# Eight state space groups in one rotation, attention masks made in the layer before, a norm emitted sooner

## The chip, the cores and the metric

The kernel runs on one core of one Trainium2 chip. The metric is the device time of one execution in microseconds (us). Five engines run side by side, each in its own fixed order of instructions: TensorE (PE, matmuls), VectorE (DVE), ScalarE (ACT), GpSimd (POOL) and SyncE (SP, which here only issues DMAs). They wait for each other by semaphores. POOL and ACT issue DMAs too, in their own instruction order.

## The reference

One layer of a decoder, for 1024 prompt tokens and 8 sample tokens that share the weights:

```
x += 1/2 * SwiGLU(RMSNorm(x))                # first FFN: 1024 -> 2816 -> 1024
h  = RMSNorm(x);  [u | q | k | v | gates] = h @ w_in
A  = S5 state space branch of u (32 groups of 16 channels, 64 complex states each), then a GLU
B  = dilated sliding window attention of q, k, v: (window, dilation) = (128,1), (512,4), (2048,16)
x += (sigmoid(gate_ssm) * (A @ w_ssm_proj) + sigmoid(gate_attn) * (B @ w_attn_proj)) @ w_o
x += 1/2 * SwiGLU(RMSNorm(x))                # second FFN
```

All in fp32. It also returns the updated key/value windows and states. The state space branch needs, for each group, tables of the powers of its 64 complex poles; they depend on weights alone. The attention needs two masks, which depend on nothing but positions.

## The kernel before

Tokens are columns: 1032 of them in three chunks of CH = 344. Features lie on the partitions, so x is three tiles xT of 128 x 8 x 344. A product in fp32 is made of three matmuls on high and low parts (`ah`/`al`, cast by ACT and subtracted by DVE, `parts` L1188).

The stages run in this order: load and first norm (`load_x` L846, nine blocks of rows: eight of 128 prompt rows, the last of 8 sample rows), first FFN up, first FFN down (`ffn_down(0)`), the mixing stage (`mix` L931: w_in products, state space, attention), the output projection and second FFN. The FFN layers use a Strassen-like scheme; its products are named P1 to P7, d1, d2, `lo` and `hi`, and each ends in four evictions on DVE (L1524) that add half of the product to xT.

Beside the products of `ffn_down(0)` the tables of the state space branch are made: after every third product `run` (L1526) calls `ssm_tables`. Its first call makes the poles (`ssm_poles` L172, many small DVE instructions on scratch tiles, result in `PO`). Each of eight further calls makes the powers for four groups on POOL, a rotation: R[128, 4, 2, 128] is filled by seven doubling steps of six instructions (L351 to L356), behind two copies (L344, L345), and is stored to DRAM (`r_d`, L358) by a DMA that POOL issues. R has one buffer, so the next rotation waits for that DMA. The call also makes other tables for the same groups on DVE and PE (L365 to L395). `ssm_inputs` (L262) makes HA, the sample states times a power, and SP stores it (`ha_d`, L315).

The masks are made by `att_setup` (L505) at the start of `mix`, in tiles of a pool of its own: one iota on POOL (L511), eight DVE instructions (L512 to L519).

The norm between the stages is `wo_norm` (L1193), once per chunk. It copies xT to DRAM (`x_d`, L1197, issued by POOL), squares on ACT (L1202, L1205), adds on DVE (L1206), sums over partitions by a matmul with ones (L1210), takes the reciprocal root (ACT L99 to L101, DVE L102 to L107), scales xT in place (L1214, which can only write when the copy to x_d has read the tile) and makes the parts for the first mixing products (L1190, L1191, then PE at L136). The w_in weights are loaded by SP (L117) into two buffers r, cast by ACT (L121) and split by DVE (L122); the next load waits for the split.

The written program gives dependences and the pools' buffers; the order on each engine is set by a scheduler that simulates the program (`schedule_with_timeline_sim=True`). So code that moves in the text shifts instructions on all engines.

## Time and profile before

| | |
|---|---|
| median of 3 runs | 2431.03 us (2425.07 to 2433.76) |
| the profiled execution | 2429.43 us, its span 2427.3 us |
| mean granted TensorE clock | 0.968 of full |
| busy: PE, DVE, ACT, POOL | 2261.9 (93%), 1559.8 (64%), 892.5 (37%), 320.5 us (13%) |

The profile is one execution. The page has the busy time of each engine, the span in 40 slices (a digit is the busy share in tenths) and the costliest groups of instructions. The timeline lists instructions with start and length; in brackets is how long the engine stood idle before one and what released it. The windows give each engine's busy time in chosen stretches. The engine with the highest share is not busy in every stretch, so one looks for the stretches where it stands.

### The profile page before, as it was taken

The numbers are of one execution on the slowest core, as the hardware profiler recorded it, in microseconds if no ns is written. First come the engines' busy times: TensorE is split into PE (matmuls) and PEld (weight loads), VectorE is DVE, ScalarE is ACT, GpSimd is POOL, SyncE is SP. The second block draws the span as 40 slices with busy tenths as digits, with TensorE's granted clock in tenths as the row PEclk, the third lists the DMA queues.
The fourth block names the chain that finished last, engine by engine and source line by source line (L and its number), as shares of the span: only waits on it lengthen the run. The fifth ranks groups of instructions, "written<-read, shape, count | busy, mean of one in ns | idle before, by whom it ended". The sixth has DMA issues, their size and how long they took to land.

```text
span 2427.3 us, 36784 instructions
## 1 busy us (share of the span) xinstructions
PE 2261.9 (93%) x14013; PEld 2162.4 (89%) x14013; DVE 1559.8 (64%) x3206; ACT 892.5 (37%) x1624; POOL 320.5 (13%) x594
## 2 busy tenths in 40 slices
PE   5999999999998079999999999899999999999999
PEld 4999999998997079987888788799999999998999
DVE  7766666679987354465557444567876666664664
ACT  6433333342221234455444443234533333333222
POOL 1000010100687710000000000120010101000000
PEclk9999999999999589999999999999999999999999
DMA  5455554577865337763143125668243434367543
GB/s 192 148 168 197 169 189 157 189 264 284 281 233 184 122 93 212 212 189 96 37 114 93 39 70 155 196 238 260 94 146 117 146 112 142 117 239 266 202 162 133
DMA packets 321830, 403.92 MB, mean 166 GB/s; under 512 B 40294, under 2 KB 266966, under 8 KB 318710
## 3 DMA queue, kind: packets, MB, share of 16 engines
q1 hardware_dynamic: 290294, 220.58, 29.8%
q0 software_dynamic: 26816, 128.54, 14.6%
q10 hardware_dynamic: 4544, 52.45, 6.3%
q8 instruction: 110, 1.80, 0.3%
q14 instruction: 66, 0.54, 0.1%
HBM read 282.62 MB, written 162.88 MB: 184 GB/s over the span
## 4 chain that ended last, share of the span: by engine, by line
PE 57%; issue 12%; DMA 11%; DVE 8%; POOL 7%; ACT 2%; SPq 2%; POOLq 0%; DVEq 0%; ACTq 0%
PE pm L1302 27%; PE pm L136 16%; PE pm L1533 9%; DMA r<-in_w_o_dram 2%; PE ps L601 2%; POOL R L356 1%; POOL q L354 1%; POOL R L353 1%; DMA r_d<-R 1%; DVE xT L1214 1%; DVE w L1191 1%; POOL q L355 1%; DMA al<-hs_d 1%; POOL hs_d L1330 1%; DMA r<-in_w_in_dram 1%
## 5 line engine op out<-in xcount | busy, mean ns | idle before, releaser
L136 PE MATMUL pm<-ah,w 128*128 128x344 f32 x1776 | 464.3, 329 | 18.9 <-ACT ah L1190 15.0
L136 PE MATMUL pm<-al,w 128*128 128x344 f32 x1632 | 439.1, 329 | 19.9 <-ACT al L1190 10.9
L1190 ACT CAST w<-r 128x1024 fp32r<-128x1024 f32 (+1 forms) x253 | 240.0, 949 | 547.6 <-PE pm L1302 349.4
L1302 PE MATMUL pm<-ah,w 128*128 128x344 f32 x2376 | 403.2, 322 | 1.0 <-ACT ah L1190 1.0
L1302 PEld LDWEIGHTS pm<-ah,w 128*128 128x128 f32 x2376 | 383.4, 190 | 1.3 <-ACT ah L1190 1.3
L136 PEld LDWEIGHTS pm<-ah,w 128*128 128x128 f32 x1776 | 315.0, 190 | 33.0 <-ACT ah L1190 15.6
L1191 DVE TENSOR_TENSOR w<-r,w 128x1024 fp32r<-128x1024 f32 (+1 forms) x253 | 277.1, 1096 | 91.1 <-ACT w L1190 90.7
L136 PEld LDWEIGHTS pm<-al,w 128*128 128x128 f32 x1632 | 294.1, 192 | 31.5 <-ACT al L1190 11.9
L1302 PE MATMUL pm<-e,w 128*128 128x344 f32 x1584 | 268.3, 322 | 14.4 <-ACT e L1190 13.4
L1302 PE MATMUL pm<-al,w 128*128 128x344 f32 x1584 | 273.9, 322 | 2.5 <-ACT p L1385 2.5
L1302 PEld LDWEIGHTS pm<-e,w 128*128 128x128 f32 x1584 | 254.5, 189 | 14.9 <-ACT e L1190 13.5
L1302 PEld LDWEIGHTS pm<-al,w 128*128 128x128 f32 x1584 | 255.7, 189 | 3.0 <-ACT p L1385 2.8
L1330 POOL DMA_DIRECT2D hs_d<-hs x110 | 75.1, 682 | 888.5 <-DVE hs L1191 840.7
L1533 PE MATMUL pm<-al,w 128*128 128x344 f32 x1068 | 183.1, 323 | 2.1 <-DVE ah L1524 2.1
L1533 PEld LDWEIGHTS pm<-al,w 128*128 128x128 f32 x1068 | 171.1, 190 | 3.7 <-DVE ah L1524 2.4
L122 DVE TENSOR_TENSOR w<-r,w 128x1024 fp32r<-128x1024 f32 (+1 forms) x58 | 60.6, 1044 | 87.0 <-ACT w L121 86.5
L1533 PE MATMUL pm<-al,x 128*128 128x344 f32 x636 | 110.9, 325 | 5.4 <-ACT ah L1541 5.0
L1533 PEld LDWEIGHTS pm<-al,x 128*128 128x128 f32 x636 | 103.1, 192 | 6.8 <-ACT ah L1541 5.3
L1127 POOL DMA_DIRECT2D rs<-g_d x24 | 12.9, 542 | 527.5 <-issue 390.4
L121 ACT CAST w<-r 128x1024 fp32r<-128x1024 f32 (+1 forms) x58 | 52.1, 898 | 74.7 <-PE pm L136 44.1
L1190 ACT CAST hs<-h 128x688 fp32r<-128x688 f32 (+1 forms) x66 | 44.1, 670 | 73.9 <-DMA hs_d<-hs 73.9
L1533 PE MATMUL pm<-e,x 128*128 128x344 f32 x360 | 65.0, 331 | 4.8 <-DVE x L1191 2.5
(427 smaller groups left out, 3279.9 us busy)
## 6 DMA issues: line engine op xcount, KB each, us to landing
hs_d<-hs POOLq DMA_DIRECT2D x88, 688.0 KB, 4.5
out_dram<-in_cache_kv_w_dram ACTq DMA_DIRECT2D x64, 512.0 KB
r<-in_w_gate_dram SPq DMA_DIRECT2D x44, 512.0 KB
r<-in_w_up_dram SPq DMA_DIRECT2D x44, 512.0 KB
al<-hs_d SPq DMA_DIRECT2D x21, 1032.0 KB
r<-in_w_in_dram SPq DMA_DIRECT2D x38, 512.0 KB
r<-in_w_down_dram SPq DMA_DIRECT2D x30, 512.0 KB
x_d<-xT POOLq DMA_DIRECT2D x9, 1376.0 KB, 7.1
```

The lines of the kernel that those rows point to most:

```text
L121: nc.scalar.copy(h[:, :k], raw[:, :k])
L122: nc.vector.tensor_sub(l[:, :k], raw[:, :k], h[:, :k])
L136: nc.tensor.matmul(p, w[:, kw], a[:, ka], start=first and i == 0, stop=last and i == n - 1)
L353: P.tensor_sub(CR[:, :, L:2 * L], q1[:, :, :L], q2[:, :, :L])
L354: P.tensor_mul(q1[:, :, :L], CR[:, :, :L], bi)
L355: P.tensor_mul(q2[:, :, :L], CI[:, :, :L], br)
L601: nc.tensor.matmul(p[h][:, :nk], qT[hs, s.block(g, b)], kT[hs, ks], start=True, stop=True)
L1190: s.nc.scalar.copy(hi, x)
L1191: s.nc.vector.tensor_sub(lo, x, hi)
L1302: nc.tensor.matmul(p, W[w][:, k], B[:, a, k], start=first and k == 0 and z == 0, stop=k == n - 1 and z == 2, skip_group_check=True)
L1330: nc.gpsimd.dma_start(s.hs_d[i:i + n, j].rearrange("i p z n -> p i (z n)"), t[:, :n].rearrange("p i z n -> p i (z n)").bitcast(F32))
L1533: nc.tensor.matmul(p[m], W[wz][:, m], t[:, jj, az], start=e == 0 and k == 0, stop=e == n - 1 and k == 2, skip_group_check=True)
```

## The change

- Rotations: only odd calls of `ssm_tables` make one, for eight groups: R[128, 8, 2, 128], 2 copies and 48 instructions (the last doubling step in two pieces of 32), one DMA of twice the bytes. Four batches replace eight.
- The poles' scratch and HA move into R's one buffer.
- `att_setup` is called at the start of `ffn_down(0)` and uses tiles rs0 to rs2 of its pool.
- `normed(0)`, the first chunk's norm, is emitted ahead of the product P3.
- `load_x` takes the sample rows seventh of nine.

```diff
--- before.py
+++ after.py
@@ -173,7 +173,16 @@
 
         nc, i = s.nc, s.i
         V = nc.vector
-        t, _ = s.ssm_pools(tp, tp)
+        RT = tp.tile([128, 8, 2, 128], F32, name="R", bufs=1).rearrange("p a b c -> p (a b c)")
+        at = [0]
+
+        def t(sh, dt=F32):
+            n = math.prod(sh[1:])
+            x = RT[:sh[0], at[0]:at[0] + n]
+            at[0] += n
+            x = x if dt == F32 else x.bitcast(dt)
+            return x if len(sh) == 2 else x.rearrange("p (a b) -> p a b", a=sh[1])
+
         s.poles(tp)
 
         a2 = t([32, 2, 128])
@@ -209,7 +218,7 @@
         V.memset(PW[:, 1, 0], 0.0)
         V.tensor_mul(PW[:, 0, 1], mag, cs)
         V.tensor_mul(PW[:, 1, 1], mag, sn)
-        m1, m2 = (tp.tile([128, 4, 64], F32, name=f"q{z}", bufs=1)[:, :, :32] for z in (1, 2))
+        m1, m2 = (tp.tile([128, 8, 32], F32, name=f"q{z}", bufs=1)[:, :4] for z in (1, 2))
 
         def cmul(outr, outi, ar, ai, br, bi, n):
             V.tensor_mul(m1[:, :n], ar, br)
@@ -295,7 +304,7 @@
         nc.sync.dma_start(s.dv, i['ssm_d'].rearrange("o (g c) -> c (o g)", c=16))
         hre = i['state_ssm_re'][0].rearrange("b g p -> (b g) p").rearrange("(q r) p -> q r p", q=2)
         him = i['state_ssm_im'][0].rearrange("b g p -> (b g) p").rearrange("(q r) p -> q r p", q=2)
-        HA = tp.tile([128, 2, 8, 32], F32, name="HA")
+        HA = tp.tile([128, 8, 2, 128], F32, name="R", bufs=1)[:, 0:2].rearrange("p a b c -> p (a b c)").rearrange("p (z b g) -> p z b g", z=2, b=8)
         HT = t(2, 256).rearrange("p (b g) -> p b g", b=8)
         for q in range(2):
             hn = t(q, 192)
@@ -337,25 +346,29 @@
             nm = names[g0 // 2 % 2][z]
             return tmp.tile([128, CH], F32, name=nm, bufs=2 if nm == "sq" else 1)[:, :sh]
 
-        sl = slice(4 * n - 4, 4 * n)
-        R = tp.tile([128, 4, 2, 128], F32, name="R", bufs=1)
-        q1, q2 = tp.tile([128, 4, 64], F32, name="q1", bufs=1), tp.tile([128, 4, 64], F32, name="q2", bufs=1)
-        CR, CI = R[:, :, 0], R[:, :, 1]
-        P.tensor_copy(CR[:, :, 0], s.ER[:, 3, sl])
-        P.tensor_copy(CI[:, :, 0], s.EI[:, 3, sl])
-        L = 1
-        while L < 128:
-            sh = [128, 4, L]
-            q = 3 + L.bit_length() - 1
-            br, bi = s.ER[:, q, sl, None].to_broadcast(sh), s.EI[:, q, sl, None].to_broadcast(sh)
-            P.tensor_mul(q1[:, :, :L], CR[:, :, :L], br)
-            P.tensor_mul(q2[:, :, :L], CI[:, :, :L], bi)
-            P.tensor_sub(CR[:, :, L:2 * L], q1[:, :, :L], q2[:, :, :L])
-            P.tensor_mul(q1[:, :, :L], CR[:, :, :L], bi)
-            P.tensor_mul(q2[:, :, :L], CI[:, :, :L], br)
-            P.tensor_add(CI[:, :, L:2 * L], q1[:, :, :L], q2[:, :, :L])
-            L *= 2
-        nc.gpsimd.dma_start(s.r_d[:, sl], R)
+        if n % 2:
+            sl = slice(4 * n - 4, 4 * n + 4)
+            R = tp.tile([128, 8, 2, 128], F32, name="R", bufs=1)
+            CR, CI = R[:, :, 0], R[:, :, 1]
+            P.tensor_copy(CR[:, :, 0], s.ER[:, 3, sl])
+            P.tensor_copy(CI[:, :, 0], s.EI[:, 3, sl])
+            L = 1
+            while L < 128:
+                q = 3 + L.bit_length() - 1
+                for l0 in range(0, L, 32):
+                    k = min(L, 32)
+                    sh = [128, 8, k]
+                    a, o = slice(l0, l0 + k), slice(L + l0, L + l0 + k)
+                    q1, q2 = (tp.tile([128, 8, 32], F32, name=f"q{z}", bufs=1)[:, :, :k] for z in (1, 2))
+                    br, bi = s.ER[:, q, sl, None].to_broadcast(sh), s.EI[:, q, sl, None].to_broadcast(sh)
+                    P.tensor_mul(q1, CR[:, :, a], br)
+                    P.tensor_mul(q2, CI[:, :, a], bi)
+                    P.tensor_sub(CR[:, :, o], q1, q2)
+                    P.tensor_mul(q1, CR[:, :, a], bi)
+                    P.tensor_mul(q2, CI[:, :, a], br)
+                    P.tensor_add(CI[:, :, o], q1, q2)
+                L *= 2
+            nc.gpsimd.dma_start(s.r_d[:, sl], R)
         for g0 in (4 * n - 4, 4 * n - 2):
             sl = slice(g0, g0 + 2)
 
@@ -505,8 +518,8 @@
     def att_setup(s, tp):
         nc = s.nc
         V = nc.vector
-        ip, ev = tp.tile([128, 256], I32, name="aip"), tp.tile([128, 128], I32, name="aev")
-        f = tp.tile([128, 256], F32, name="aif")
+        ip, ev, f = (tp.tile([128, CH], F32, name=f"rs{z}", bufs=1) for z in range(3))
+        ip, ev, f = ip[:, :256].bitcast(I32), ev[:, :128].bitcast(I32), f[:, :256]
         s.m12, s.m3 = s.cst.tile([128, 256], F32, name="m12"), s.cst.tile([128, 128], F32, name="m3")
         nc.gpsimd.iota(ip, pattern=[[-1, 256]], base=128, channel_multiplier=1)
         V.tensor_copy(f, ip)
@@ -847,7 +860,7 @@
 
         nc = s.nc
         R, N = {}, []
-        for b in range(9):
+        for b in (0, 1, 2, 3, 4, 5, 8, 6, 7):
             n = 128 if b < 8 else 8
             xr = tmp.tile([128, D], F32, name="xr", bufs=XB)
             nc.sync.dma_start(xr[:n], s.i['x_prompt'][0, 128 * b:128 * b + 128, :] if b < 8 else s.i['x_sample'][:, 0, :])
@@ -877,7 +890,7 @@
                     nc.tensor.transpose(p[:, k, :n], xr[:n, (hf * 4 + k) * 128:(hf * 4 + k + 1) * 128], s.ident[:n, :n])
                 for c, cs, bs in pieces:
                     nc.scalar.copy(xT[c][:, 4 * hf:4 * hf + 4, cs], p[:, :, bs])
-            if b in (2, 5, 8):
+            if b in (2, 5, 7):
                 r = tmp2.tile([128, CH], F32, name=f"rs{b // 3}", bufs=1)
                 nc.scalar.copy(r, R[b // 3][:, :CH])
                 N.append(s.wo_norm(tmp2, xT, b // 3, 0, r))
@@ -956,8 +969,6 @@
                     with ExitStack() as c:
                         psum(c, 3, 5)
                         s.pn = s.pt
-                        with ExitStack() as c_:
-                            s.att_setup(pool(c_, "atmp"))
                         up, kp = pool(c, "up"), pool(c, "kp")
                         s.ssm_setup(kp)
                         sp = pool(c, "sp", 2)
@@ -1483,6 +1494,7 @@
             for c, (x, y) in zip((1, 2, 0), (('P2', 'P4'), ('P3', 'P5'), ('lo', 'hi'))):
                 two_of(xT[c].rearrange("p (a k) n -> p a k n", a=2), x, y)
             tmp, stp = pool(ctx, "tmp", 2), pool(ctx, "stp")
+            s.att_setup(tmp)
         two_of(sl('ah0'), 'P1', 'P6')
         two_of(sl('ah1'), 'P7', 'x')
         HI = {'P5': 0, 'P6': 1, 'P7': 2, 'P4': 3, 'P1': 4, 'd1': 5, 'P2': 6, 'P3': 7, 'd2': 8}
@@ -1667,8 +1679,8 @@
             td = hload('d1'), hload('d2')
             if not z:
                 A21 = ops(0, half1, "ws")
+            normed(0)
             run(W, 'P3')
-            normed(0)
             out(1, 0, 'P3')
             if z:
                 A21 = ops(0, half1, "ws")
```

Line numbers of the changed kernel are higher: the copies of a rotation are L353 and L354, its steps L364 to L369, its DMA L371, the iota L524, evictions L1536, the norm L1208 (x_d), L1217 (adds) and L1225 (scaling).

POOL before, from inside the seventh rotation over the iota to the start of the eighth (R is the rotations' tile, aip the iota's, x_d takes the copies of xT; another x_d stands at 344, a third at 364):

```order
347 L1197 DMA x_d<-xT_4902 128x2752
348 L356 TENSOR_TENSOR R<-q_7526,q_7527 128x4x32
349 L351 TENSOR_TENSOR q_7526<-R,PO 128x256
350 L352 TENSOR_TENSOR q_7527<-R,PO 128x256
351 L353 TENSOR_TENSOR R<-q_7526,q_7527 128x4x64
352 L354 TENSOR_TENSOR q_7526<-R,PO 128x256
353 L355 TENSOR_TENSOR q_7527<-R,PO 128x256
354 L356 TENSOR_TENSOR R<-q_7526,q_7527 128x4x64
355 L358 DMA r_d<-R 128x1024
356 L511 IOTA aip 128x256
357 L344 COPY R<-PO 128x4
```

POOL after, at the first rotation and behind the fourth:

```order
38 L1341 DMA hs_d<-hs 128x688
39 L524 IOTA rs_4909 128x256
40 L353 COPY R<-PO 128x8
41 L354 COPY R<-PO 128x8
42 L364 TENSOR_TENSOR q_5575<-R,PO 128x8
```

```order
242 L369 TENSOR_TENSOR R<-q_7492,q_7493 128x8x32
243 L371 DMA r_d<-R 128x2048
244 L1208 DMA x_d<-xT_4901 128x2752
245 L1208 DMA x_d<-xT_4902 128x2752
246 L1208 DMA x_d<-xT_4900 128x2752
```

The iota now stands ahead of all rotations, and the three copies to x_d behind all of them; before, two stood within the seventh and one within the eighth.

DVE before, at the end of the first FFN (xT_4900 takes the last evictions, rs is the norm's sum, aif and aev the mask tiles):

```order
1194 L1524 SCALAR_TENSOR_TENSOR xT_4900<-pm,xT_4900 128x344 x3
1195 L512 CAST aif<-aip 128x256
1196 L516 TENSOR_SCALAR aev<-aip 128x128
1197 L513 TENSOR_SCALAR m_8621<-aif 128x256
1198 L517 CAST m_8622<-aev 128x128
1199 L514 TENSOR_SCALAR aif<-aif 128x256
1200 L518 TENSOR_SCALAR m_8622<-m_8622 128x128
1201 L515 TENSOR_TENSOR m_8621<-m_8621,aif 128x256
1202 L519 TENSOR_TENSOR m_8622<-m_8622,m_8621 128x128
1203 L1206 TENSOR_TENSOR rs_8320<-rs_8320,sq 128x344
1204 L122 TENSOR_TENSOR w_8652<-r_8648,w_8651 128x1024
1205 L1206 TENSOR_TENSOR rs_8320<-rs_8320,sq 128x344 x2
```

DVE after, at the same place:

```order
1201 L1536 SCALAR_TENSOR_TENSOR xT_4900<-pm,xT_4900 128x344 x4
1202 L1217 TENSOR_TENSOR rs_8168<-rs_8168,sq 128x344 x6
1203 L122 TENSOR_TENSOR w_8514<-r_8510,w_8513 128x1024
1204 L1217 TENSOR_TENSOR rs_8168<-rs_8168,sq 128x344
1205 L1536 SCALAR_TENSOR_TENSOR xT_4900<-pm,xT_4900 128x344 x4
1206 L122 TENSOR_TENSOR w_8521<-r_8517,w_8520 128x1024
1207 L102 TENSOR_TENSOR rs_8193<-rs_8193,rs_8195 128x344
1208 L103 TENSOR_SCALAR rs_8196<-rs_8193 128x344
1209 L122 TENSOR_TENSOR w_8708<-r_8704,w_8707 128x1024
```

The mask instructions are gone from here, and the norm's adds stand between the `lo` and `hi` evictions; a weight split (L122) stands between L103 and L104.

SP before, around the store of HA (al and ah are operand loads for the products):

```order
97 L1505 DMA al_6371<-hs_d 128x3x688
98 L315 DMA ha_d<-HA 128x512
99 L1505 DMA al_6133<-hs_d 128x3x688
100 L1505 DMA ah_6191<-hs_d 128x3x688
101 L390 DMA b_d<-sq 128x256
```

SP after, at the same place, where HA lies in R:

```order
98 L1517 DMA al_6355<-hs_d 128x3x688
99 L1517 DMA al_6097<-hs_d 128x3x688
100 L1517 DMA ah_6155<-hs_d 128x3x688
101 L1517 DMA al_6413<-hs_d 128x3x688
102 L324 DMA ha_d<-R 128x512
103 L1517 DMA al_6477<-hs_d 128x3x688
```

The store of HA moved behind three more operand loads, one of which stood two rows behind it before.

## Rows read from the trace of the kernel before

**Rows 1.** The page: PE's busy time, and PE in 40 equal slices of the span.

```profile
PE 2261.9 (93%) x14013; PEld 2162.4 (89%) x14013; DVE 1559.8 (64%) x3206; ACT 892.5 (37%) x1624; POOL 320.5 (13%) x594
...
PE   5999999999998079999999999899999999999999
```

**Rows 2.** Windows: stretch, length, busy of PE, PEld, DVE, ACT, POOL, clock, DMA share.

```profile
622.00:700.00 78.00, 77.34 (x484) 72.41 (x483) 71.76 (x209) 16.55 (x30) 64.69 (x130) 1.00 0.84 272
700.00:760.00 60.00, 57.22 (x353) 53.57 (x351) 56.42 (x144) 15.31 (x27) 47.95 (x54) 0.99 0.58 191
760.00:786.00 26.00, 23.89 (x133) 21.32 (x132) 14.27 (x33) 1.63 (x4) 20.14 (x41) 0.90 0.50 162
786.00:833.00 47.00, 0.00 (x0) 0.00 (x0) 7.53 (x20) 3.22 (x7) 32.46 (x101) 0.53 0.27 105
833.00:846.00 13.00, 1.88 (x3) 0.87 (x4) 9.38 (x16) 7.12 (x10) 11.48 (x30) 0.50 0.67 229
```

**Rows 3.** Timeline of PE: start, length, engine, line, tiles, count, [idle before <-releaser].

```profile
783.83 2.06 PE L1533 MATMUL pm<-al,w 128*128 128x344 f32 x12
...
833.25 1.52 PE L1210 MATMUL pT<-rs,ones 128*128 128x344 f32 x2 [47.37 <-DVE rs L1206]
845.63 0.94 PE L136 MATMUL pm<-al,w 128*128 128x344 f32 x2 [10.87 <-ACT al L1190]
```

**Rows 4.** Timeline of DVE around the hole.

```profile
777.44 1.46 DVE L1524 SCALAR_TENSOR_TENSOR xT<-pm,xT 128x344 f32<-128x344 f32 x3 [0.87 <-PE pm L1533]
825.23 0.29 DVE L512 CAST aif<-aip 128x256 f32<-128x256 int32 x1 [46.32 <-POOL aip L511]
...
826.91 0.51 DVE L1206 TENSOR_TENSOR rs<-rs,sq 128x344 f32<-128x344 f32 x1
...
832.06 1.13 DVE L1206 TENSOR_TENSOR rs<-rs,sq 128x344 f32<-128x344 f32 x2
...
842.03 4.75 DVE L1214 SCALAR_TENSOR_TENSOR xT<-xT,gains,rs 128x344 f32<-128x344 f32 x8
```

**Rows 5.** Timeline of POOL: rotations, their DMA, the iota.

```profile
622.66 0.20 POOL L351 TENSOR_TENSOR q<-R,PO 128x4 f32<-128x4 f32 x1 [62.24 <-DVE PO L220]
...
658.19 5.84 POOL L354 TENSOR_TENSOR q<-R,PO 128x64 f32<-128x64 f32 x1
...
788.85 0.18 POOL L344 COPY R<-PO 128x4 f32<-128x4 f32 x1 [6.38 <-DMA r_d<-R]
...
790.56 0.20 POOL L351 TENSOR_TENSOR q<-R,PO 128x8 f32<-128x8 f32 x1
...
799.99 0.61 POOL L351 TENSOR_TENSOR q<-R,PO 128x256 f32<-128x256 f32 x1
...
804.34 0.59 POOL L358 DMA_DIRECT2D r_d<-R  x1 [0.30 <-POOL R L356]
...
824.83 0.36 POOL L511 IOTA aip<- 128x256 int32 x1
```

**Rows 6.** Windows at the kernel's start: the last idle stretch before the full work.

```profile
49.60:63.00 13.40, 0.03 (x1) 0.00 (x0) 12.86 (x14) 5.79 (x5) 0.00 (x0) 0.59 0.00 0
63.00:66.00 3.00, 2.94 (x10) 2.94 (x11) 3.00 (x3) 1.33 (x2) 0.00 (x0) 0.50 0.00 0
```

**Rows 7.** Waits: who <- whom: us in total, times, longest us.

```profile
POOL R L344 <- DMA r_d<-R: 26.0, 7, 6.4
```

**Rows 8.** Timeline of SP and DVE: a split load, the 23rd eviction, weight loads.

```profile
599.51 6.04 SPq L1505 DMA_DIRECT2D al<-hs_d  x2
...
601.23 0.50 DVE L1524 SCALAR_TENSOR_TENSOR ah<-pm,ah 128x344 f32<-128x344 f32 x1
...
828.58 21.70 SPq L117 DMA_DIRECT2D r<-in_w_in_dram  x4
```

**Rows 9.** The copies to x_d (L1197) in 780 to 860, by line.

```profile
DMA to landing us min/median/max: 5.0/5.1/7.1
```

## The prediction

> **What bounds the kernel now.** I read the page first: PE is busy 93% of the span, and the strip of 40 slices is full except for the start and two slices past a third of the span [rows 1]. So the time is PE's work plus the holes in it, and only a change that closes or opens a hole counts. The windows show the hole: PE does nothing from 786 to 833 and 1.88 us in the next 13 [rows 2]. The timeline of PE gives its edges: the second layer's last products start at 783.83 and end at 785.89, the ones-matmul of the first norm runs at 833.25, the first mixing product at 845.63 [rows 3]. That is 59.7 us without a product.
>
> The waits in brackets say who caused it. PE waited 47.4 us for L1206, the adds of the norm's squares [rows 3], and DVE itself stood 46.3 us at L512, a cast of the iota tile: the last `lo` evictions ended at 778.90, and then the masks stood at DVE's head until 825.23 [rows 4]. POOL made the iota at 824.83, directly behind the seventh rotation's DMA [rows 5]. So the hole is DVE's mask work queued ahead of the norm, and behind POOL's rotations.
>
> **The change part by part.** The sum is made against the profiled execution, 2429.43 us (span 2427.3, and 2.1 around it); the median of the runs is 2431.03, 1.6 higher.
>
> *Masks early, first norm sooner.* The iota now stands ahead of all rotations on POOL, and the eight mask instructions stand among the pole work at the start of the layer. In order on DVE now: four `lo` evictions, six L1206, a weight split (L122), the seventh L1206, four `hi` evictions. The `lo` evictions end at 778.90, as in before. The seven L1206 with a weight split and four evictions took 833.19 - 826.91 = 6.3 us in before; the evictions are gone, but ACT's squares set the pace too; I keep 6.3 and get 785.2 [rows 4]. PE's products end at 785.89, so the ones-matmul can start there, not at 833.25: 47.4 us earlier. From the ones-matmul to the first mixing product before took 845.63 - 833.25 = 12.4 us: rsqrt steps, scaling, split. I keep it, with two corrections. The ones-matmul runs at the higher clock, -0.8. A weight split (L122) stands in the middle of the rsqrt steps as one did before, but its weight load is now released by the split between the adds, at about 786, and must land before the square root's steps are over, some 5 us later: 0 to 4 us, taken at 1.5. PE then resumes at 785.9 + 13.1 = 799.0 instead of 845.6: **-46.6 us**. What is late next is the rsqrt chain itself, and behind it x_d (below).
>
> The clock: after the hole PE ran at 0.50 of full (1.2 GHz) [rows 2], and at the start of the kernel, after only 13.4 us idle, it also ran at 0.50 for the next 3 us [rows 6]. The new hole is 13 us, so I count no gain from the clock.
>
> *Mask work at its new place.* 826.91 - 825.23 = 1.7 us of DVE [rows 4]. Beside pole work that PE doesn't wait for, 0; if it holds an eviction back, up to 1.7. Taken as 0.5.
>
> *Rotations.* One undisturbed rotation of four groups takes 804.34 - 0.30 - 788.85 = 15.2 us (the 0.30 is what its DMA stood idle); the two copies and the first step of six instructions take 1.7, the last step (256 elements an instruction) 804.04 - 799.99 = 4.05 [rows 5]. A rotation of eight groups has the same steps on twice the elements, with the last one in two pieces: it loses the step of four elements (1.4 without the copies) and gains two of 4.05, 21.9 us. Beside a busy DVE it is longer: in 622 to 786 POOL's 225 instructions were busy 64.69 + 47.95 + 20.14 = 132.8 us, 0.59 each, and in 786 to 833, with DVE nearly idle, 101 took 32.46, 0.32 each [rows 2]. By instruction that is 0.27 us more for each: four rotations, 4 x (21.9 + 50 x 0.27) = 142 us. By proportion it is 4 x 21.9 x 1.84 = 161. With the worst stretch (47.95/54 = 0.89, so 0.57 more), 4 x (21.9 + 28.4) = 201. Below, undisturbed: 88. Three waits for R's DMA between them, at most 6.4 us each for half the bytes [rows 7]: 19. So 107 to 220, likely 161 to 180.
>
> One row decides between the two readings: a 128x64 instruction that takes less than the 0.7 us of a 256-element one (4.05 us for six) took 5.84 at 658.19 [rows 5], so what is paid is a wait and not a slower element; I lean to the lower figure and take 170 with the DMA waits. The Trainium skill says the same of the kind of it ("SBUF — State Buffer", SBUF: two separate sides): the port pair that the two engines share is an exclusive lock for a whole instruction. It would make each wait no longer than one DVE instruction; the 5.84 us here spans many of DVE's, so the measurement decides, and by the rule (half of an add's 0.51 us [rows 4], 50 times) the four would take 139 us instead of 142, and the sum stays as it is.
>
> *When the first rotation starts.* R has one buffer, and it now holds first the poles' scratch, then HA, then the rotations. HA's last instruction stood at twelve evictions before, and now stands behind 23; the 23rd was at 601.23 [rows 8]. Its DMA now stands on SP behind the load that went at 599.51 (the first of the two in that row) [rows 8]. So it goes at about 602 and lands in 5 us, by the nearest rows (0.25 MB against the 5.0 to 7.1 of a larger one [rows 9]): 607. Before, the first rotation could run only at 622.66, when the poles were done [rows 5]. So four rotations run from 607 to 777 (714 to 827), and nothing on POOL waits for PE between.
>
> *x_d.* Its three DMAs follow the rotations on POOL, at 0.6 us each, and land in 5.0 to 7.1 us [rows 9]; the scaling (L1214) of the first norm can't write before. The first is issued at 777 to 778 and lands by 785, with the loads beside it perhaps by 790. The scaling is due at 785.9 + (842.03 - 833.25) = 794.7 [rows 3, 4]. So it is covered by 5 to 10 us: cost 0, range 0 to +40.
>
> *Table work and evictions in another order.* The same DVE instructions, with up to 13 us fewer of them ahead of PE's evictions between 620 and 680, and up to 4 us more between 756 and 770 (counted along the new order with the trace's mean duration of each line). PE's idle time in 622 to 786 is 0.7 + 2.8 + 2.1 = 5.6 us [rows 2], so no more than that can come back; the end, where DVE is full, may lose 4. Taken as +0.5.
>
> *Sample rows seventh.* The same nine blocks; the last norm's chain at the start, which holds PE 13.4 us [rows 6], has its small block out of the way earlier. 0 to -3, taken as -1.
>
> Sum: 2429.4 - 46.6 + 0.5 + 0.5 - 1 = **2383 us**. Behind the mixing products the order of every engine is the same as before, and from about 891 PE is full, so the gain passes through.
>
> **The rivals.**
> 1. *The copy to x_d comes late.* Everything of POOL now stands ahead of x_d: four rotations, where before two copies slipped in beside the seventh. If the rotations take more than 180 us (worst stretch 220), the scaling waits: at 200 us x_d lands at 607 + 200 + 7 = 814, 19 us past 794.7, 2402 us; at 220, 2422. For: DVE is nearly full in 700 to 760, and POOL got 54 instructions done there [rows 2]. Against: that is the worst stretch of four. The Trainium skill has a rule for this place (same page and section): a DMA issued from GpSimd can't have its descriptors written while DVE runs certain instructions, so it seems blocked. Before, the third x_d was issued beside the norm's adds and a weight split, and none of the three took over 7.1 us to land [rows 9], so the trace doesn't bear it out. Chance 0.17.
> 2. *More comes back.* With fewer POOL instructions to collide with and the early products freer, PE's small holes in the layer close too, and the rsqrt chain runs without POOL beside it: another 5 to 10 us, about 2374. Against: the holes are only 5.6 us. Chance 0.10.
> 3. *No gain*, because the first mixing products turn out to wait for their weights: the loads of w_in went out at 828.58 [rows 8]. But they were released by the weight split at 827, which stood behind the masks, so they move along. 2429. Chance 0.04.
> 4. *Slower.* One buffer for scratch, HA and the rotations makes a chain: poles, HA, its DMA, four rotations, x_d, scaling. It decides when x_d lands after 842, where the scaling stood before: with 170 us of rotations the first one must start after 665 instead of 607, or with the start at 607 they must take 228. For: the poles were done only at 622 before, and they share DVE with evictions and tables. Against: now they stand ahead of much table work. At a start of 680 x_d lands at 857, 15 us late: 2445. Chance 0.05.
>
> **How the numbers follow.** Forecast 0.64, rivals 0.17, 0.10, 0.04, 0.05. The time is the forecast's, 2383; its own range, with the load (0 to 4), the start (0 to -3) and the table work (-4 to +4), is 2377 to 2391. To hold 8 in 10 it takes in rival 2 in part and rival 1 up to about 2406: 2370 to 2406. A measurement of this kernel can tell about 0.3%, 7 us, from no change. Forecast and rivals 1 and 2 are faster: 0.90; rival 3 and the tail of rival 1 the same: 0.05; rival 4: 0.05.
>
> **What would show it.** In the new profile: the hole in PE from about 786 to 799; no wait of DVE at the masks; L1206 directly behind the `lo` evictions; four rotations starting near 607 and ending before 790; x_d landed before the scaling starts, so that the scaling follows the last rsqrt step without a wait. Wrong would be: a wait of the scaling on x_d's DMA (rival 1), the first rotation after 650 (rival 4), or a first mixing product that waits for a weight load (rival 3).

## The result, and the profile after

The changed kernel took 2415.87 us (median of 8 runs, 2402.51 to 2422.29) against 2435.39 us for the kernel before (8 runs, 2425.07 to 2440.62): a ratio of 0.9916, 95% interval 0.9890 to 0.9941. It is about 20 us faster. The prediction said 2383, about 47 us faster, with a range of 2370 to 2406; the direction was right and the time lies 10 us outside the range. The profiled executions are 2429.43 us before and 2415.39 us after, a difference of 14.0 us.

The page of the kernel after answers to [rows 1]: the empty slice past a third of the span now reads 6, and two slices ahead of it (7 and 8) that were full are not any more.

```profile
PE 2268.1 (94%) x14013; PEld 2164.9 (90%) x14013; DVE 1573.5 (65%) x3206; ACT 890.6 (37%) x1624; POOL 283.0 (12%) x438
...
PE   5999999979989679989999999899999999999999
```

PE's timeline of the kernel after (start, length, line, tiles, [idle before <-releaser]), against [rows 3]:

```profile
545.34 1.23 PE L1545 MATMUL pm<-al,x 128*128 128x344 f32 x3 [15.53 <-ACT ah L1553]
...
657.59 4.57 PE L1545 MATMUL pm<-al,w 128*128 128x344 f32 x17 [3.96 <-ACT w L1201]
...
821.59 2.06 PE L1545 MATMUL pm<-al,w 128*128 128x344 f32 x12
823.56 0.84 PE L1221 MATMUL pT<-rs,ones 128*128 128x344 f32 x2
835.42 0.94 PE L136 MATMUL pm<-al,w 128*128 128x344 f32 x2 [11.02 <-ACT al L1201]
```

The ones-matmul now stands directly behind the layer's last product, without a wait. From the end of the products (823.6) to the first mixing product (835.4) it is 11.8 us, where it was 59.7: 47.9 us came back in the hole of this profile, as forecast. But the products end at 823.6 and not at 785.9: the layer itself became 37.7 us longer. The first mixing product starts 10.2 us earlier than before; the other 3.8 of the 14.0 us come back behind it, by difference.

The windows of the kernel after (columns as in [rows 2]) show the longer layer; the last two rows are the new hole and the 13 us behind it:

```profile
622.00:700.00 78.00, 68.46 (x407) 62.44 (x406) 68.23 (x175) 15.34 (x30) 61.19 (x86) 0.97 0.72 236
700.00:760.00 60.00, 57.99 (x355) 53.97 (x354) 55.43 (x166) 13.74 (x25) 42.11 (x73) 0.98 0.69 236
760.00:786.00 26.00, 20.31 (x121) 17.65 (x120) 26.00 (x52) 5.22 (x9) 24.90 (x22) 0.96 0.60 195
515.00:824.00 309.00, 266.43 (x1566) 247.61 (x1564) 265.64 (x808) 66.63 (x129) 151.74 (x211) 0.93 0.71 237
...
824.40:835.40 11.00, 0.00 (x1) 0.00 (x0) 9.23 (x18) 5.67 (x8) 0.53 (x1) 0.68 0.99 314
835.40:848.40 13.00, 11.04 (x50) 10.08 (x50) 8.21 (x12) 7.71 (x13) 0.15 (x1) 0.75 0.15 42
```

In 760 to 786 DVE is busy all the time, where it was busy 14.27 of 26 us before [rows 2]; PE idles beside it. The whole layer before, from 515 to 786, has this row:

```profile
515.00:786.00 271.00, 256.35 (x1564) 241.12 (x1563) 241.15 (x790) 64.20 (x120) 135.86 (x229) 0.97 0.75 253
```

PE does the same products in both (x1564 and x1566), but DVE's busy time rose from 241.15 to 265.64 us for nearly the same count of instructions (in the second are the masks and the norm's first adds), and PE's idle time from 14.7 to 42.6 us. The other 10 us of the longer layer are PE's busy time, 266.43 us and not 256.35, at a mean granted clock of 0.93 and not 0.97: after the stand of 15.53 us above, for one, it was 0.66 from 545 to 550 and 1.00 from 550 to 560. Two things in the trace can be behind the waits. The first is POOL: its waits and its timeline (against [rows 5, 7]) show four rotations inside the layer, starting at 616.0, 656.8, 707.1 and 741.5.

```profile
POOL R L353 <- DMA r_d<-R: 26.3, 3, 11.0
```

```profile
533.46 0.34 POOL L524 IOTA rs<- 128x256 int32 x1 [0.59 <-DMA hs_d<-hs]
...
615.96 0.57 POOL L353 COPY R<-PO 128x8 f32<-128x8 f32 x1 [82.16 <-DVE w L1202]
...
656.76 0.19 POOL L353 COPY R<-PO 128x8 f32<-128x8 f32 x1 [10.97 <-DMA r_d<-R]
...
795.52 4.38 POOL L369 TENSOR_TENSOR R<-q,q 128x256 f32<-128x256 f32 x1
800.20 0.59 POOL L371 DMA_DIRECT2D r_d<-R  x1 [0.30 <-POOL R L369]
803.08 0.53 POOL L1208 DMA_DIRECT2D x_d<-xT  x1 [2.30 <-DVE xT L1536]
```

The second is ACT, which the prediction didn't look at. It issues copies of the cache to the output, six in a row, and its evictions stand behind them in order:

```profile
531.02 13.77 ACTq L811 DMA_DIRECT2D out_dram<-in_cache_kv_w_dram  x6
544.83 0.81 ACT L1553 ACTIVATE ah<-pm 128x344 f32<-128x344 f32 x2 [13.36 <-DMA B<-in_ssm_b_re_dram]
...
643.24 13.64 ACTq L811 DMA_DIRECT2D out_dram<-in_cache_kv_w_dram  x5
656.92 0.62 ACT L1201 CAST w<-r 128x512 fp32r<-128x512 f32 x1 [13.79 <-DMA out_dram<-in_cache_kv_w_dram]
```

PE's waits at 545.34 (15.53 us) and 657.59 (3.96 us) end on exactly these instructions, and behind the second DVE stood 9.29 us as well. The name in the first bracket is another DMA that came last; the row above it shows where ACT stood. Before, the same copies took 4.07 and 5.38 us:

```profile
530.29 4.07 ACTq L798 DMA_DIRECT2D out_dram<-in_cache_kv_w_dram  x6
...
613.38 5.38 ACTq L798 DMA_DIRECT2D out_dram<-in_cache_kv_w_dram  x6
```

### The profile page after: what moved, and what is told of

Same layout as the page of the kernel before. It is cut to its first block, busy times and chain, and to the rows that moved or that the text cites. A ratio compares the mean times of both kernels' runs of the same rounds, so it can differ in the third digit from the quotient of the medians.

```text
span 2413.6 us, 36624 instructions
## 1 busy us (share of the span) xinstructions
PE 2268.1 (94%) x14013; PEld 2164.9 (90%) x14013; DVE 1573.5 (65%) x3206; ACT 890.6 (37%) x1624; POOL 283.0 (12%) x438
## 3 DMA queue, kind: packets, MB, share of 16 engines
q0 software_dynamic: 26240, 128.54, 14.7%
## 4 chain that ended last, share of the span: by engine, by line
PE 63%; DVE 13%; DMA 11%; issue 7%; ACT 2%; SPq 2%; POOL 1%; ACTq 0%; DVEq 0%; POOLq 0%
PE pm L1313 31%; PE pm L136 16%; PE pm L1545 10%; DMA r<-in_w_o_dram 2%; DVE w L1202 2%; PE ps L614 2%; DMA r<-in_w_down_dram 1%; DVE xT L1225 1%; PE acc L630 1%; DVE xT L1536 1%; PE pT L623 1%; DMA b_d<-sq 1%; PE pn L932 1%; ACT w L1201 1%; DMA r<-in_w_in_dram 1%
## 5 line engine op out<-in xcount | busy, mean ns | idle before, releaser
L1313 PE MATMUL pm<-e,w 128*128 128x344 f32 x1584 | 266.5, 320 | 14.4 <-ACT e L1201 13.3
L1313 PEld LDWEIGHTS pm<-al,w 128*128 128x128 f32 x1584 | 255.2, 188 | 3.3 <-ACT p L1396 2.8
L1545 PE MATMUL pm<-al,x 128*128 128x344 f32 x636 | 111.8, 327 | 17.1 <-ACT ah L1553 15.5
L122 DVE TENSOR_TENSOR w<-r,w 128x1024 fp32r<-128x1024 f32 (+1 forms) x58 | 60.2, 1039 | 90.5 <-ACT w L121 80.0
L1545 PE MATMUL pm<-e,w 128*128 128x344 f32 x384 | 68.1, 321 | 1.2 <-DVE ah L1536 1.2
```

Source lines behind the costliest of these rows:

```text
L122: nc.vector.tensor_sub(l[:, :k], raw[:, :k], h[:, :k])
L1313: nc.tensor.matmul(p, W[w][:, k], B[:, a, k], start=first and k == 0 and z == 0, stop=k == n - 1 and z == 2, skip_group_check=True)
L1545: nc.tensor.matmul(p[m], W[wz][:, m], t[:, jj, az], start=e == 0 and k == 0, stop=e == n - 1 and k == 2, skip_group_check=True)
```

## The experiments

Two theories of the longer layer were tested against each other. **R**: the rotations cost. Before, three of the eight ran in the hole (12 of 32 groups), beside an idle DVE; now all run beside DVE's table work and hold it up. **C**: ACT's copies cost. A third question was which part of the change earns the 20 us. "Layer end" is the end of the layer's last product (in e5, e9 and e12 small products of the tables come last, 2 to 5 us behind the others), "mixing" the start of the first mixing product, both from one profile each. "Copies" are ACT's cache copies, "there" is the first FFN down, and "x_d from SP" means that SP issues the copies of xT. Each ratio is to runs of the kernel before in the same session; their medians were 2432.0 to 2433.3 us for e1 to e12.

| kernel | median us | ratio to before | layer end | mixing |
|---|---|---|---|---|
| before, profiled three times | 2435.39 | - | 785.9, 800.8, 794.0 | 845.6, 858.2, 851.1 |
| after | 2415.87 | 0.9916 (0.9890 to 0.9941) | 823.6 | 835.4 |
| e4 after again | 2415.74 | 0.9928 (0.9901 to 0.9954) | 822.3 | 843.4 |
| e3 after, no rotations | 2395.73 | 0.9845 (0.9815 to 0.9874) | 802.9 | 822.3 |
| e5 after, no copies in the layer's first pass | 2415.73 | 0.9930 (0.9910 to 0.9950) | 800.6 | 834.8 |
| e9 after, neither | 2390.24 | 0.9827 (0.9803 to 0.9851) | 784.6 | 811.0 |
| e8 after, fourth rotation in the hole | 2411.51 | 0.9910 (0.9890 to 0.9929) | 816.3 | 827.5 |
| e6 before, no copies there | 2422.67 | 0.9959 (0.9943 to 0.9976) | 776.3 | 822.0 |
| e1 masks, norm, sample rows alone | 2431.96 | 0.9990 (0.9970 to 1.0011) | 803.6 | 852.8 |
| e7 e1, x_d from SP | 2412.60 | 0.9908 (0.9882 to 0.9934) | 804.2 | 819.3 |
| e11 e7, no copies there | 2421.44 | 0.9952 (0.9932 to 0.9972) | 784.4 | 789.4 |
| e10 eight-group rotations alone | 2419.11 | 0.9939 (0.9918 to 0.9961) | 822.9 | 844.7 |
| e2 after with four-group rotations | 2437.45 | 1.0013 (0.9992 to 1.0034) | 809.8 | 841.3 |
| e12 after, x_d from SP, no copies there | 2403.09 | 0.9882 (0.9856 to 0.9908) | 796.0 | 818.3 |

**Without the rotations (e3).** The kernel after, with the rotations' arithmetic left out; R only gets zeros and is stored. The whole block of a rotation goes (two of its lines are shown):

```diff
-            P.tensor_copy(CR[:, :, 0], s.ER[:, 3, sl])
...
-                    P.tensor_add(CI[:, :, o], q1, q2)
+            P.memset(R, 0.0)
```

> The whole change, but the 50 rotation instructions of each batch are left out: R is only set to zero by one POOL instruction and stored, four times. If POOL's instructions beside DVE cost the layer time (A1), it ends 15 to 28 us earlier, 2388 to 2400; if the loss is in the early stall on ACT's copies and in the order (A2, B), the time stays within 6 us of the whole change.

The layer ended 20.7 us earlier, and the median is 20.1 us lower than after's. (The profiled execution is e3's slowest, 2405.71 us, 9.7 below after's.) DVE shows why. These are groups by line in the layer (count | busy us, mean ns | idle us), first of the kernel after, then of before, then of e3; the first row of each is the 128x256 addition (its mean mixes in a second shape), the other two are the same two 128x32 multiplies.

```profile
L391 DVE TENSOR_TENSOR rs<-rs,rs 128x256 f32<-128x256 f32 (+1 forms) x16 | 8.9, 557 | 0.0
L378 DVE TENSOR_TENSOR b<-B,PO 128x32 f32<-128x32 f32 x16 | 5.6, 348 | 0.0
L382 DVE TENSOR_TENSOR b<-B,PO 128x32 f32<-128x32 f32 x16 | 5.2, 333 | 0.0
```

```profile
L378 DVE TENSOR_TENSOR rs<-rs,rs 128x256 f32<-128x256 f32 (+1 forms) x16 | 6.9, 433 | 0.0
...
L365 DVE TENSOR_TENSOR b<-B,PO 128x32 f32<-128x32 f32 x16 | 3.5, 219 | 1.3 <-PE pT L387 1.3
...
L369 DVE TENSOR_TENSOR b<-B,PO 128x32 f32<-128x32 f32 x16 | 3.0, 194 | 0.0
```

```profile
L373 DVE TENSOR_TENSOR rs<-rs,rs 128x256 f32<-128x256 f32 (+1 forms) x16 | 6.9, 430 | 0.1
...
L360 DVE TENSOR_TENSOR b<-B,PO 128x32 f32<-128x32 f32 x16 | 2.9, 182 | 2.0 <-PE pT L382 2.0
...
L364 DVE TENSOR_TENSOR b<-B,PO 128x32 f32<-128x32 f32 x16 | 2.7, 174 | 0.0
```

The first multiply costs DVE 182 ns on the mean with POOL nearly still, 219 beside before's rotations and 348 beside the new ones. The second profile of the kernel after (e4) has 240 for it, 287 for the second multiply and 484 for the addition, so the size differs between executions and the sign doesn't. From after to e3 only POOL's work changes, so this is a price that DVE pays for POOL. The prediction used the Trainium skill's rule for one half of this alone ("SBUF — State Buffer", SBUF: two separate sides): the lock on the shared port pair makes whichever engine comes second stand, so POOL's long instructions hold DVE's short ones too. The rows agree with that half, in sign.

The number of rotations alone doesn't explain the price. The five that before had inside the layer cost DVE little: its busy time was 241.2, 245.6 and 243.7 us in the three profiles, against 238.8 without any. In e2, with six and most of a seventh rotation of four groups inside the layer, it was 255.2. Whether the larger instructions or the place where they fall matters more is not shown.

**Without the copies (e5), and without both (e9).** The edit of e5; e9 is e3 and e5 together:

```diff
-                    s.shift()
+                    if z:
+                        s.shift()
```

> The changed kernel, but ACT issues none of its cache copies (DRAM to DRAM) during the first FFN down; they go out later. Theory: in the changed kernel ACT stands 13.8 and 13.6 us at two groups of these copies (4.1, 5.4 and 4.3 before), since SP's many small transfers for the tables fill the path at the same moment; PE lost about 10 us at the first and up to 9 at the second. Then the waits of PE for ACT near 545 and 658 go, the layer ends near 805 instead of 823, and the time falls to about 2400 (-10 to -18). If DVE is the bound of the layer anyway, it gives back less than 6.

> The changed kernel without the rotations' arithmetic (R set to zero and stored) and with ACT's cache copies moved out of the layer: both suspected costs taken away together. Alone each ended the layer near 800 to 803 (no rotation 802.7, no copies about 800) against 823. If the two are separate costs, about 20 us each, and nothing else is wrong with the new order, the layer ends at 785 or earlier and the whole is about 2380, what was predicted. If they are one cost (a late DVE in both), it ends near 800 and the whole is about 2396.

The layer ended 23.0 us earlier in e5, and 39.0 in e9, at 784.6. The two costs are separate, 20.7 and 23.0 us with 5 in common, and taking both away gives the layer's end that the forecast had (785.9). The time is still 2390.24 us, 7 over the forecast, since the mixing starts at 811.0 and not at 799.0 (below). The windows of the layer in e3, e5 and e9 (columns as above) confirm which cost sits where:

```profile
515.00:803.00 288.00, 258.84 (x1561) 240.65 (x1560) 238.79 (x800) 64.01 (x121) 13.54 (x15) 0.96 0.76 254
```

```profile
515.00:801.00 286.00, 260.29 (x1560) 240.24 (x1558) 265.73 (x800) 63.69 (x120) 153.00 (x212) 0.98 0.63 209
```

```profile
515.00:785.00 270.00, 252.66 (x1559) 237.66 (x1558) 237.52 (x795) 61.91 (x118) 13.50 (x15) 0.99 0.70 229
```

DVE's busy time is 265.7 us with rotations, copies or not (257.0 in e4), and 238 to 239 without: 18 to 27 us of DVE for theory R alone. The copies leave DVE's busy time as it is and add to PE's waits.

Yet e5's median is the same as after's. What it won was lost again at the norm, as DVE's timeline of e5 shows:

```profile
816.16 1.23 DVE L122 TENSOR_TENSOR w<-r,w 128x1024 fp32r<-128x1024 f32 x1 [15.47 <-ACT w L121]
...
817.64 0.49 DVE L1217 TENSOR_TENSOR rs<-rs,sq 128x344 f32<-128x344 f32 x1
```

and PE's:

```profile
823.71 1.52 PE L1221 MATMUL pT<-rs,ones 128*128 128x344 f32 x2 [23.13 <-DVE rs L1217]
834.82 0.94 PE L136 MATMUL pm<-al,w 128*128 128x344 f32 x2 [9.59 <-ACT al L1201]
```

A weight split stands ahead of the norm's adds on DVE, and ACT waited 15.62 us for its load. The DMA engines were full in that time (share 1.02 from 800 to 815), with the three x_d copies, issued at 795.5 to 799.5 (14.2 us to land, 6.3 in the kernel after), among the transfers; that these copies hold the load is likely and not shown. The load is the one that rival 3 named, but here it holds the adds and not the first mixing product. In e9 the ones-matmul waited too, 15.36 us, and there 5.6 us had another cause: the squares on ACT write tiles rs and sq, which the tables use as well, and had to wait for the stores from them.

```profile
792.02 0.49 ACT L1195 ACTIVATE rs<-xT 128x344 f32<-128x344 f32 x1 [2.86 <-DMA b_d<-rs]
...
796.34 0.87 ACT L1198 ACTIVATE sq<-xT 128x344 f32<-128x344 f32 x2 [2.76 <-DMA b_d<-sq]
```

**One rotation back in the hole (e8).** The fourth rotation begins with a small copy that reads the last eviction:

```diff
+        if gate is not None:
+            P.tensor_copy(CR[:, 0, 0:4], gate)
...
+                s.rotate(stp, 7, xT[RC[2]][:, 7, :4])
```

> The changed kernel with the fourth rotation held back until the last eviction of the layer (one tiny POOL copy that reads its result gates it), so that three rotations run beside DVE and one in the hole behind. Theory: what POOL does beside DVE costs the layer about 20 us for four rotations (no rotation: 2396 against 2416), so 5 to 8 us come back: the layer ends at 815 to 818, 2408 to 2411. If the fourth rotation is what the tables' end waits for, or the norm suffers, it is 2416 or slower.

The layer ended 7.4 us earlier than after, the mixing started 7.9 earlier, and the median fell 4.4 us, with intervals that overlap. In size it fits a quarter of e3's effect or a little more; by itself it would prove little.

**The parts alone (e1, e10).** e1 is the kernel before with the masks, the norm and the sample rows of the change; e10 is the kernel before with the rotations alone. The edit of e1, in parts (its mask tiles also move to rs0 to rs2):

```diff
-        for b in range(9):
+        for b in (0, 1, 2, 3, 4, 5, 8, 6, 7):
...
-                        with ExitStack() as c_:
-                            s.att_setup(pool(c_, "atmp"))
...
+            s.att_setup(tmp)
...
+            normed(0)
             run(W, 'P3')
-            normed(0)
```

> The kernel before with three parts of the change alone: masks made in the layer, first norm ahead of P3, sample rows seventh. Rotations stay at four groups, poles' scratch and HA keep tiles of their own. Theory A (what the layer lost, some 38 us, comes from the parts on R: eight groups an instruction, and scratch and HA in R's buffer): the hole closes and the layer ends near 786, so about 2383 to 2392 us, the last product of the layer at 786 to 792. Theory B (what it lost comes from the early masks and the new order of the scheduler): about 2415, as the whole change.

> The kernel before with the rotations part alone (eight groups an instruction, scratch and HA in R); masks, norm and sample rows as before. The iota then stands behind four longer rotations and not behind seven. Theory: POOL is done with them near 785 to 800, as in the changed kernel, so the masks come 25 to 35 us earlier than at 824 and most of the gain is in this part: about 2410 to 2420. If the layer grows by as much as the hole shrinks, about 2432.

e1 gains nothing, which neither of its theories said, and e10 gains 0.6%. In e1 PE waited only 1.73 us for the adds, nearly as in the prediction; then the wait moved on to x_d. Rows of e1 on POOL, DVE and PE:

```profile
842.66 0.58 POOL L358 DMA_DIRECT2D r_d<-R  x1 [0.30 <-POOL R L356]
843.25 1.08 POOL L1195 DMA_DIRECT2D x_d<-xT  x2
```

```profile
849.28 3.99 DVE L1212 SCALAR_TENSOR_TENSOR xT<-xT,gains,rs 128x344 f32<-128x344 f32 x8 [35.81 <-DMA x_d<-xT]
```

```profile
852.75 0.94 PE L136 MATMUL pm<-al,w 128*128 128x344 f32 x2 [46.58 <-ACT al L1188]
```

With the old rotations POOL reaches the x_d copies only at 843.25, behind the seventh of eight, and the hole is still 49.2 us. In e10 POOL was done by 802.70, so the iota, still in its old place, came at 815.54, and the masks no longer held the norm long: PE waited 4.73 us for the adds, and the whole hole was 21.8 us. So in before and in e1 the hole lasts until POOL is through with its rotations, seven of the eight; what the eight groups buy is that POOL is through 42 us earlier (800.2 in after, 842.7 in e1).

**x_d from SP (e7, e11, e12).** If that reading is right, e1 must gain once x_d doesn't stand behind POOL:

```diff
-        nc.gpsimd.dma_start(s.x_d[c], xT[c])
+        (nc.sync if z == 1 else nc.gpsimd).dma_start(s.x_d[c], xT[c])
```

> The first experiment (masks early, norm sooner, sample rows seventh; rotations of four groups, own scratch) with one more edit: the copies to x_d before the first norm are issued by SP and not by POOL. There the first mixing product waited until 852.8, since x_d stood behind seven rotations on POOL (issued at 843.2). Theory: the scaling then follows the square root at once, the first mixing product is at about 818 to 822, and the time falls by about 30 to some 2400. If the rotations themselves (r_d) are needed soon after, it is 2415 or more.

It did: mixing at 819.3 instead of 852.8, and 19.4 us less in the median, as much as the whole change, with the old rotations. That is less than the 33.5 us at the mixing, and 12 us over what was expected. e11, which takes the copies out as well, shows where the rest goes.

> A version built from the findings: rotations of four groups with own scratch, masks early, norm sooner, sample rows seventh, x_d issued by SP, ACT's cache copies out of the layer. The layer should end near 785 to 795 (before without copies: 776; with x_d on SP: 804), the first mixing product 14 us later: 2390 to 2400. If the weight loads wait behind the copies to x_d as in the fifth experiment, about 2412.

The hole shrank to 5 us, with mixing at 789.4, but the kernel was slower than e7, 2421.44 us where 2390 to 2400 was expected. The rotations left over now run beside the mixing, until 893.7. A small POOL instruction of the state space branch (L423) stands behind the seventh of them, SP waits for it at a load, and SP's next stores, of u, are what ACT and then PE wait for: PE stood 31.16 us until 888.44. SP's wait in e11:

```profile
SPq L426 <- POOL U L423: 32.9, 1, 32.9
```

In e7 the same wait is 13.7 us on SP, and PE stood 12.07 us until 896.09. e12 makes both edits of e11 in the kernel after, whose rotations end in time.

> The whole change with x_d issued by SP and ACT's cache copies out of the layer. In the fifth experiment the layer ended near 800 but a weight load stood 15.6 us behind the three copies to x_d that were issued together; on SP the first two can go out as soon as their chunks are ready. Theory: the first mixing product at about 815 and 2393 to 2400. If the third copy on SP holds the weight loads behind it, about 2412.

At 2403.09 us it has the lowest median of the versions that compute everything, 12.8 us below after's median (measured in another session; the intervals of the two ratios just overlap) and 3 us over what was expected. PE's timeline of e12, and a row of ACT, show what is left: the adds wait for squares, and these, as in e9, for the store from a table tile.

```profile
807.23 1.52 PE L1221 MATMUL pT<-rs,ones 128*128 128x344 f32 x2 [11.21 <-DVE rs L1217]
818.32 0.94 PE L136 MATMUL pm<-al,w 128*128 128x344 f32 x2 [9.58 <-ACT al L1201]
```

```profile
802.41 0.87 ACT L1216 ACTIVATE sq<-xT 128x344 f32<-128x344 f32 x2 [4.59 <-DMA c_d<-sq]
```

**Is the long stand of the copies the change's doing? (e4, e6, e13, e14)** The kernels after (e4) and before (e13 and e14, one execution each, 2434.38 and 2432.93 us) were profiled again unchanged, and e6 is the kernel before with e5's edit.

> The changed kernel once more, on the same chip as the three others: 2416 within 7 us. If the wait of PE for ACT near 545 (15.5 us in the first profile, 5.0 before) is a chance of DMA timing, it may be shorter here; if it comes from the program's order, it is again 13 to 16 us.

> The kernel before with the same edit. In its profile the first group took 4.1 us; if the long stall is the rule only with the new order, this is 2425 to 2432, within 5 us of the kernel before. If it strikes in some executions of the kernel before too (its times spread from 2422 to 2441), the median falls by 5 to 10 us and the spread narrows.

> The kernel before, profiled again. If the long stand at the first group of ACT's copies is the changed order's doing, the group takes 4 to 5 us again and the layer's last product ends within 2 us of 785.9. If it is chance, one of two more profiles shows 11 to 14 us at some group of copies and the layer ends 5 to 15 us later.

> The kernel before, profiled a third time, with the same two readings as for the second: 4 to 5 us at the first group of copies if the stand belongs to the changed order, 11 to 14 us at some group in one of the two if it is chance.

The first group took 4.07 us in the profile of before that the prediction read, 4.11 in e14, and in e13:

```profile
529.94 14.76 ACTq L798 DMA_DIRECT2D out_dram<-in_cache_kv_w_dram  x6
```

So the first long stand comes in before too, in one profile of three; in after it came in both. The second (13.64 us in after, 14.21 in e4, 14.53 in e10, 11.17 in e2) came in every profile with the eight groups or the scratch in R and with rotations, 7.40 us in e3, and in before, e1 and e7 it never passed 5.38. A third group took 11.19 us in after and 4.57 in e4. In before, taking the copies out gains 0.4% (e6), and its layer ends at 776.3; but the spread of the times didn't narrow (17.7 us, 15.5 for before), so e6 doesn't show that the first stand is what it took away.

Of the 37.7 us that the layer lost between the two profiles, some 10 are thus that one profile's luck (PE waited 5.02 us there at 534.92, and 15.53 in after). The three profiles of before end the layer at 793.6 on the mean and the two of the changed kernel at 823.0, 29 us later. The hole has its luck too. In e4 a fourth group took 8.30 us at 809.32 (3.74 in after), the store b_d from tile rs, issued at 808.89, landed only at 825.09, and the first square of the norm waited for it:

```profile
825.09 0.49 ACT L1213 ACTIVATE rs<-xT 128x344 f32<-128x344 f32 x1 [15.42 <-DMA b_d<-rs]
```

So e4's hole is 21.1 us, not 11.8. The medians, 20 us apart, are a better measure than the profiles' 14.

**Four groups in the new buffer (e2).** The kernel after with the old rotation in half of R, scratch and HA still in R.

```diff
-        if n % 2:
-            sl = slice(4 * n - 4, 4 * n + 4)
...
+        sl = slice(4 * n - 4, 4 * n)
+        R = tp.tile([128, 8, 2, 128], F32, name="R", bufs=1)[:, :4]
```

> The whole change, but rotations of four groups at a time (in half of R), eight of them; scratch and HA stay in R. Theory A1 (POOL's instructions on eight groups hold DVE's two-input table instructions longer: L378 went from 0.45 to 0.57 us each, DVE's busy time in the layer rose by some 17 us): about 2395 to 2400, mean of the table instructions back to before's. Theory A2 (scratch in R makes the poles' loads go 3.4 us later, and ACT's copies then stand 13.8 us instead of 4.1): still about 2410, the wait of PE for ACT at 545 stays at 15 us.

Neither theory is met. The gain is gone, which says again that it is the eight groups' doing: even in its profile x_d stands behind rotations again (two copies issued at 836.20), and PE waited 24.24 us until the mixing at 841.3. But its profiled execution took 2418.66 us, 19 us less than the median of its runs, so its rows don't explain the median, and this run carries no more than that. The opposite, eight groups with their own scratch, wasn't tried, so what the scratch and HA in R cost by themselves is not shown.

## Why the prediction was wrong

*Masks and norm, -46.6.* The mechanism was right, and the number came out in part by luck. The masks stand at the layer's start, the adds directly behind the `lo` evictions (816.96 behind 814.71), the chain of the norm took 11.8 us from the last product, and the hole gave back 47.9. In e4, the same kernel, it gave back 38.6, and in e9, where the layer ends as early as forecast, 33.3: there the mixing started at 811.0 and not at the sum's 799.0. The sum had nothing for the squares' wait for stores of table tiles, and 1.5 us for a weight load. The clock gave next to nothing, as said: 0.75 of full in the 13 us from the first mixing product, and 0.68 in the same 13 us of before (845.6 to 858.6).

*x_d, 0.* Right, on DVE's timeline of after: the scaling followed the last step without a wait, 8.4 us after the ones-matmul started (8.8 in [rows 3, 4]).

```profile
814.71 1.94 DVE L1536 SCALAR_TENSOR_TENSOR xT<-pm,xT 128x344 f32<-128x344 f32 x4 [2.86 <-PE pm L1545]
816.96 0.52 DVE L1217 TENSOR_TENSOR rs<-rs,sq 128x344 f32<-128x344 f32 x1 [0.31 <-ACT sq L1216]
...
831.96 3.99 DVE L1225 SCALAR_TENSOR_TENSOR xT<-xT,gains,rs 128x344 f32<-128x344 f32 x8
```

But the late end of the layer helped: the rotations ended at 800.2, and a copy issued then would have landed after the forecast's 794.7. How late the rotations would end in a layer without its delays, no run shows. Rival 1's mechanism was real: in e1 the scaling waited 35.81 us for x_d.

*Four rotations, 170 us from 607.* They started at 616 and took 184, within the range given. The start was late since HA's last instruction ran at 613.2, not 602, behind the 10 us that the layer had already lost at ACT's first copies.

*Table work and evictions: "the end, where DVE is full, may lose 4. Taken as +0.5."* **This step failed.** It counted DVE's instructions in the new order "with the trace's mean duration of each line", means taken while 12 of the 32 groups were still to run in the hole, and in smaller instructions. With all 32 beside DVE the three means above rose by 29 to 72% in one profile and by 10 to 48% in the other, and e3 puts POOL's work at 20.7 us of the layer and 20 us of the time (a small part of that was in the means already: before's own rotations cost DVE 2 to 7 us). The prediction asked what DVE does to POOL and priced that carefully (0.27 us an instruction); it never asked what POOL does to DVE, though DVE was busy 241.15 of the layer's 271 us.

A second cost is missing from the sum altogether: no term looks at ACT's queue. It was taken as running as before, and in the trace at hand its copies took 4 and 5 us. Without them the layer ended 23.0 us earlier (e5), but the time fell only with a second edit (no rotations in e9, 5.5 us under e3; x_d from SP in e12, 12.8 us under after), since the norm lost it again. That the first stand comes in before too could not be read from one profile; the second comes with the change.

*Rivals.* The 2416 us look like rival 1's 2402 to 2422, but it is not its mechanism: nothing waited for x_d. Rival 2 (more comes back) was wrong in sign, and rival 4's late first rotation (after 650) didn't come: it started at 616. The forecast's own range, added up from its parts, is 2375 to 2390 and not 2377 to 2391; nothing hangs on that.

**Open:** what the second group of copies stands for on ACT. Shown is that it goes with the copies and not that a certain transfer causes it; that the layer's loads and the rotations' DMA share the engines with it (DMA share 0.72 in 622 to 700) is only a thought. POOL, in the same stretch, waited up to 11.0 us for r_d (6.4 before). Open too is whether the change makes the first long stand likelier: it came in after, e4, e1, e3, e7, e8 and e10, not in e2, and in one of three profiles of before.

## What to carry to other kernels

Work that an engine does inside a stall is free only while the stall lasts: whoever closes the stall must put that work somewhere, and price it on both engines, the one that does it and the one that runs beside it. In a layer where DVE is 89% busy, means per instruction from the old order are not the means of the new one. One profile can hold a stand of 10 us that the next doesn't, so a term read from one needs a second. Behind a wait of 47 us look for the next in line on every queue (here POOL's x_d), and read also the engines that the change doesn't touch, their DMA issues above all.

## What was not expected of the hardware

- Beside the rotations of eight groups a two-tile multiply of DVE (128x32, float32) took 348 ns on the mean (240 in e4), 182 without them, and the 128x256 addition 557 (484), 430 without. POOL's own last rotation instruction took 4.38 us at 795.52; the same instruction took 0.87 to 0.91 us at 634 to 645.
- Six DMA issues of 512 KB on ACT took 4.07 us in one profile and 14.76 in another of the same kernel, before; why is open. In after ACT's next evictions came only behind them (13.77 us, then the eviction at 544.83).
- The copies to x_d landed in 6.3 us (median) in the kernel after, and in 14.2 in e5, where three were issued within 4 us beside weight loads.
